# Idle TensorE products in the head of a macaron encoder layer, and its first loads in another order

## The chip, the core and the metric

One core of a Trainium2 chip runs the kernel. The time is that of one execution on the device, in microseconds (us); lower is better. The engines of the core run side by side, each with its own queue of instructions: TensorE (PE in the profile, PEld its weight loads) multiplies, VectorE (DVE) and ScalarE (ACT) do elementwise work, GpSimd (POOL) and SyncE (SP) mostly issue transfers (DMAs). An instruction waits at the head of its engine's queue until what it needs is there, and what is queued behind it waits too.

## What is computed

A layer on x of 1024 tokens by 1024 features, in float32: a half-step SwiGLU FFN, an attention block with two groups of heads, and a second half-step FFN, each between two RMS norms. The change touches only the start of the first FFN:

```python
def rmsnorm(x, g):
    xf = x.astype(jnp.float32)
    y = xf * lax.rsqrt(jnp.mean(xf * xf, axis=-1, keepdims=True) + NORM_EPS)
    return (y * g.astype(jnp.float32)).astype(x.dtype)

def swiglu(x, w_gate, w_up, w_down):
    return (jax.nn.silu(x @ w_gate) * (x @ w_up)) @ w_down
...
h = swiglu(rmsnorm(x, ffn1_pre_g[l]), ffn1_w_gate[l], ffn1_w_up[l], ffn1_w_down[l])
x = x + 0.5 * rmsnorm(h, ffn1_post_g[l])
```

## The kernel before

The matrix products run by a Strassen-like scheme on 512-wide blocks, and every operand is split into a rounded part (hi) and a rest (lo), so that one product of blocks is three matmuls: hi by hi (L466), hi by the rest of x (L467), rest by hi (L472). The four first tiles of x (128 rows each, 1024 columns) make the left operand of the first block.

The head does this. SP and ACT load tiles 0 and 1 of x in halves (L1637), the gain's row `ffn1_pre_g` (L1639, SP), then half blocks of two weights (L1647, L1651), tiles 2 and 3 of x (L1648 on ACT, L1649 on SP) and a third weight (L1652). The gain has to stand in all 128 partitions: `spread_gain` multiplies a row of ones (stationary, 1x128) by the gain's row (1x512, twice) on TensorE (L344, tile `gps`), and ACT copies the two results (L345). Meanwhile ACT and DVE square and sum the tiles (L166, L1665), and `rstd_by_sqrt` with `newton` make 1/rms for a pair of tiles (tile y, called r0 for tiles 0 and 1 and r1 for 2 and 3). `scaled` multiplies x by y and by the gain (L1672, tile xn), `transposed` turns it in blocks of 128x128 on TensorE (L174, tile trp), ACT rounds the result to hi (L181), DVE takes the rest (L182). Then the first products run (`pg.mm`, L466, L467, L472) on the columns of tiles 0 and 1 alone (256 wide). Tiles 2 and 3 follow with the same steps, and the products on the other 256 columns. ACT also splits the weights (L1683, with DVE L1686) and copies transposed blocks (L261) to be stored by POOL (L262).

In this head the order on TensorE, DVE and ACT is that in which the code is written (`ordered(DVE, ACT)`); SP and POOL issue their transfers in program order, and a transfer whose semaphore is still in use by an earlier one waits for it. The PSUM tiles of gps, of the products and of the tiles that the change adds come in turn from one pool of six banks (tag "mm"); those of the transposes have their own pool (L174).

`make_identity` fills c.ident (128x128), the stationary or moving operand of a transpose, on POOL at the start. xn[0] and xn[1] are the tiles that later hold the normalised tiles 0 and 1; before that, the gain's row lies in row 0 of xn[0] and the ones in xn[1].

Of the kernel before, what the change touches and what calls it, by code (L numbers as in the profile page):

```python
# [10 lines left out]
F32 = mybir.dt.float32  # L11
# [8 lines left out]
P, T = 128, 512  # L20
# [82 lines left out]
class Weights:  # L103
# [30 lines left out]
    def next(self):  # L134
        return self.ready.popleft()
# [180 lines left out]
def newton(c, y, e, h):  # L316

    nc = c.nc
    nc.vector.reciprocal(y, e)
    nc.vector.scalar_tensor_tensor(e, y, -1.0, h, op0=ALU.mult, op1=ALU.mult)  # L320
    nc.vector.tensor_mul(e, e, y)
    nc.vector.scalar_tensor_tensor(y, e, 1.5, y, op0=ALU.add, op1=ALU.mult)
    return y


def rstd_by_sqrt(c, ss):

    nc, k = c.nc, ss.shape[1]
    h, y, e = [c.small.tile([P, 4], F32, tag=t, name=t)[:, :k] for t in ("v", "y", "e")]
    nc.vector.tensor_add(h, ss[:, :, 0], ss[:, :, 1])  # L330
    nc.vector.tensor_scalar(h, h, 0.5 / D, 0.5 * EPS, op0=ALU.mult, op1=ALU.add)
    nc.scalar.activation(e, h, AF.Sqrt, scale=2.0)
    yield
    yield newton(c, y, e, h)


def spread_gain(c, t, row, one):

    nc = c.nc
    copies = []  # L340
    for h in range(2):
        sl = slice(h * T, h * T + T)
        ps = c.psm.tile([P, T], F32, tag="mm", name="gps")
        nc.tensor.matmul(ps, one, row[:, sl], start=True, stop=True)  # L344
        copies.append(lambda sl=sl, ps=ps: nc.scalar.copy(t[:, sl], ps))  # L345
    return t, *copies
# [1052 lines left out]
def layer(tc, a, out):  # L1399
    nc = tc.nc  # L1400
    c = Ctx(tc)
    with ExitStack() as ctx:
# [26 lines left out]
        x0 = [a["x"][t * P:(t + 1) * P, :] for t in range(8)]  # L1429
# [51 lines left out]
        def gate_pairs(which, op, wg, wu, early):  # L1481
            return PairGemm(c, op, [(wg[f], wu[f]) for f in range(NF)], early, GatePairs(c, which))

        def ffn(which, op, prep, pg, get, turns, sums, more, post, pre, src, dst, begin=None, tables=()):
# [7 lines left out]
            if begin:  # L1492
                left_pool(e)
            begun = begin(pg) if begin else ()
            plan(pg.early, turns)
            r = sub()
# [119 lines left out]
        with ExitStack() as order:  # L1616
# [9 lines left out]
            half = [slice(0, T), slice(T, D)]  # L1626
            first_junk = [c.xp.tile([P, D], F32, tag="s", name="junk", bufs=2)]
            w2 = c.xp.tile([P, D], F32, tag="x1", name="w2", bufs=2)
            xn = [c.xp.tile([P, D], F32, tag="xn", name="xn", bufs=c.xn) for _ in range(2)]
            gain = c.xp.tile([P, D], F32, tag="pre", name="gain", bufs=1)  # L1630
            xs = {t: c.xp.tile([P, D], F32, tag="x", name="x", bufs=4) for t in range(4)}
            xn += [xs[2], xs[3]]
            op0 = Operand(c, None, 0)
            nc.gpsimd.memset(xn[1][:1, :P], 1.0)
            for t in range(2):
                for h, q in enumerate((nc.sync, nc.scalar)):
                    q.dma_start(xs[t][:, half[h]], x0[t][:, half[h]])  # L1637
                    if (t, h) == (0, 0):
                        nc.sync.dma_start(xn[0][:1], a["ffn1_pre_g"])  # L1639
            op0.gain, *gains = spread_gain(c, gain, xn[0][:1], xn[1][:1, :P])  # L1640

            def begin(pg):
                for b in range(2):
                    pg.raw[b] = c.wg.tile([P, 2, T], F32, tag="g", name="graw")
                pg.raw[2] = w2.rearrange("p (i x) -> p i x", i=2)
                for b in range(2):
                    nc.sync.dma_start(pg.raw[b][:, 0], pg.srcs[b][0][:, half[0]])  # L1647
                nc.scalar.dma_start(xs[2], x0[2])  # L1648
                nc.sync.dma_start(xs[3], x0[3])  # L1649
                for b in range(2):  # L1650
                    nc.sync.dma_start(pg.raw[b][:, 1], pg.srcs[b][0][:, half[1]])  # L1651
# [6 lines left out]
                def square(t, h=None, to=None):  # L1658

                    x = xs[t] if h is None else xs[t][:, half[h]]  # L1660
                    acc = ss[t // 2][:, t % 2, h or 0:(h or 0) + 1]
                    if to is None:
                        sumsq(c, x, acc, junk()[:, :x.shape[1]])
                    else:
                        nc.vector.tensor_tensor_reduce(out=to, in0=x, in1=x, scale=1.0, scalar=0.0,  # L1665
                                                       op0=ALU.mult, op1=ALU.add, accum_out=acc)

                def scaled(r, h, *ts):

                    for t in ts:  # L1670
                        sl = half[h]
                        nc.vector.scalar_tensor_tensor(xn[t][:, sl], xs[t][:, sl], r[:, t % 2:t % 2 + 1],  # L1672
                                                       op0.gain[:, sl], op0=ALU.mult, op1=ALU.mult)
                        if not h:
                            op0.parts[t] = deque(((A11, xn[t][:, :T]), (A12, xn[t][:, T:])))
# [25 lines left out]
                gains[1]()  # L1701
                square(2)
                r0 = next(root)
                scaled(r0, 0, 0, 1)
                lo0(0)
                keeps = []
                op0.one(0, keeps)
                op0.one(1, keeps)
                hi1(0)
                square(3, 0)  # L1710
                square(3, 1, junk()[:, half[1]])
                root = rstd_by_sqrt(c, ss[1])
                next(root)
                lo1(0)
# [57 lines left out]
            pg = PairGemm(c, op, [(a["wqk"][p], a["wqk"][8 + p]) for p in QK_ORDER], 8, QKPairs(c))  # L1772
# [163 lines left out]
        with ordered():  # L1936
# [18 lines left out]
            pg = gate_pairs(3, op, a["wg2"], a["wu2"], 11)  # L1955
# [94 lines left out]
```

## Time and profile before

| what | value |
|---|---|
| median of 3 runs | 1828.1 us (1826.97 to 1828.38) |
| the profiled execution | 1828.32 us |
| its span, first to last instruction | 1826.5 us |
| mean granted TensorE clock | 0.999 |

The span in 40 equal slices (about 46 us each); each digit is the busy share in tenths, PEclk the granted TensorE clock, DMA the mean busy share of the 16 DMA engines:

```profile
PE   8999999999999999999999999999999999999998
PEclk9999999999999999999999999999999999999999
DMA  7756566557888858868687523594655566596564
```

TensorE is full but in the first and the last slice. The change works in the first 20 us, less than half of the first slice. A matmul's record is longer than its step: matmuls overlap, so the pace is read from start to start. A float32 product that isn't of the rounded kind (L344) leaves two records, each with a weight load.

### The profile page before, as it was taken

What the parts mean: (1) busy time and instruction counts of PE and PEld (TensorE: products, weight loads), DVE (VectorE), ACT (ScalarE), POOL (GpSimd) and SP (SyncE); (2) the same over time, 40 slices, a digit from 0 to 9 for tenths busy, and PEclk for the clock granted to TensorE, in tenths of its full rate; (3) what the DMA queues carried; (4) which work ended last, traced back from release to release, by engine and by line L of the source; (5) the groups of instructions that cost most, each with busy time, mean ns of one, the idle gap of its engine ahead of it and who ended that gap; (6) DMA issues with size and microseconds to landing.
All of it is one profiled execution on the core that took longest, in us unless ns stands there. A gap on an engine that the chain in (4) does not pass through costs nothing.

```text
span 1826.5 us, 25169 instructions
## 1 busy us (share of the span) xinstructions
PE 1808.7 (99%) x8876; PEld 1522.9 (83%) x8876; DVE 1309.8 (72%) x2225; ACT 832.1 (46%) x1495; POOL 352.3 (19%) x583
## 2 busy tenths in 40 slices
PE   8999999999999999999999999999999999999998
PEld 6888888888888888888999998888888888888886
DVE  6878877776466878477666856778877777664557
ACT  6622233334443656234688765654223333354433
POOL 2223321112021123232344100221111111110000
PEclk9999999999999999999999999999999999999999
DMA  7756566557888858868687523594655566596564
GB/s 277 263 182 215 166 226 224 203 208 260 306 302 307 288 200 265 265 226 294 198 264 254 184 97 116 192 309 162 196 179 196 201 221 223 185 349 196 193 230 143
DMA packets 172769, 409.28 MB, mean 224 GB/s; under 512 B 20401, under 2 KB 42321, under 8 KB 170594
## 3 DMA queue, kind: packets, MB, share of 16 engines
q1 hardware_dynamic: 124450, 246.07, 40.9%
q0 software_dynamic: 47184, 159.51, 24.0%
q10 hardware_dynamic: 1008, 2.10, 0.3%
q8 instruction: 70, 1.15, 0.3%
q14 instruction: 57, 0.47, 0.1%
HBM read 280.09 MB, written 132.56 MB: 226 GB/s over the span
## 4 chain that ended last, share of the span: by engine, by line
PE 92%; DVE 3%; DMA 2%; ACT 1%; issue 1%; SPq 0%; DVEq 0%; ACTq 0%
PE accp L783 26%; PE mmp L467 17%; PE mmp L466 17%; PE mmp L472 17%; PE po L1215 2%; PE ptp L1095 2%; PE po L1331 2%; PE accp L357 1%; PE accp L359 1%; PE accp L358 1%; PE sp L1182 1%; PE trp L174 1%; PE sp L1315 1%; DMA praw<-in_wd_dram 1%; DMA graw<-in_wg_dram 1%
## 5 line engine op out<-in xcount | busy, mean ns | idle before, releaser
L466 PE MATMUL mmp<-x,whi 128*128 128x512 f32 (+1 forms) x1464 | 571.8, 391 | 1.7 <-ACT x L181 1.4
L467 PE MATMUL mmp<-x,whi 128*128 128x512 f32 (+1 forms) x1464 | 569.2, 389 | 0.8 <-DVE x L182 0.7
L783 PE MATMUL accp<-pw 128*128 128x512 f32 x1800 | 411.2, 390 | 0.4 <-ACT hb L804 0.4
L783 PEld LDWEIGHTS accp<-pw 128*128 128x128 f32 x1800 | 337.2, 188 | 70.5 <-ACT hb L804 0.8
L472 PE MATMUL mmp<-x,wlo 128*128 128x512 f32 (+1 forms) x1464 | 390.6, 389 | 0.0
L466 PEld LDWEIGHTS mmp<-x,whi 128*128 128x128 f32 x1464 | 275.7, 188 | 59.6 <-ACT x L181 2.2
L467 PEld LDWEIGHTS mmp<-x,whi 128*128 128x128 f32 x1464 | 275.7, 188 | 57.4 <-DVE x L182 1.6
L472 PEld LDWEIGHTS mmp<-x,wlo 128*128 128x128 f32 x1464 | 274.7, 188 | 56.8
L751 DVE TENSOR_TENSOR pw<-praw,pw 128x1024 fp32r<-128x1024 f32 (+1 forms) x181 | 201.2, 1150 | 126.0 <-ACT pw L750 125.1
L750 ACT CAST pw<-praw 128x1024 fp32r<-128x1024 f32 (+1 forms) x181 | 168.8, 983 | 207.4 <-PE accp L783 162.6
L456 ACT CAST whi<-wraw 128x1024 fp32r<-128x1024 f32 x126 | 132.7, 1053 | 187.5 <-PE mmp L467 161.9
L457 DVE TENSOR_TENSOR wlo<-wraw,whi 128x1024 fp32r<-128x1024 f32 x126 | 153.3, 1218 | 2.5 <-ACT whi L456 2.5
L693 POOL DMA_DIRECT2D g<-sg x44 | 24.0, 545 | 428.5 <-DVE sg L686 243.0
L481 ACT COPY s<-mmp 128x512 f32<-128x512 f32 x52 | 30.6, 589 | 131.3 <-PE mmp L472 121.5
L456 ACT CAST whi<-traw 128x512 fp32r<-128x512 f32 x52 | 32.3, 621 | 122.9 <-DVE traw L554 100.0
L645 DVE TENSOR_TENSOR c<-mmp,u 128x512 f32<-128x512 f32 x52 | 35.9, 691 | 69.9 <-PE mmp L472 69.8
L553 DVE TENSOR_TENSOR wraw<-wraw 128x1024 f32<-128x1024 f32 x52 | 63.6, 1224 | 18.1 <-DMA wraw<-in_wu_dram 17.2
L783 PE MATMUL accp<-pw,x 128*128 128x512 f32 x312 | 71.8, 390 | 0.0
L1085 DVE CUSTOM_DVE_ANT_0 s<-sp,g 128x256 f32<-128x256 f32 (+1 forms) x128 | 48.3, 413 | 30.2 <-PE sp L1182 24.5
L783 PEld LDWEIGHTS accp<-pw,x 128*128 128x128 f32 x312 | 58.3, 188 | 12.4 <-DVE pw L751 0.3
L632 DVE TENSOR_TENSOR c<-mmp,v 128x512 f32<-128x512 f32 x52 | 35.8, 689 | 34.1 <-PE mmp L472 34.0
L1331 PE MATMUL po<-vs,pt 128*128 128x128 f32 x352 | 49.9, 276 | 0.0
(280 smaller groups left out, 2489.8 us busy)
## 6 DMA issues: line engine op xcount, KB each, us to landing
praw<-g SPq DMA_DIRECT2D x70, 512.0 KB
wraw<-in_wg_dram SPq DMA_DIRECT2D x44, 512.0 KB
wraw<-in_wu_dram SPq DMA_DIRECT2D x44, 512.0 KB
tr<-in_wd_dram SPq DMA_DIRECT2D x44, 512.0 KB
g<-sg POOLq DMA_DIRECT2D x88, 256.0 KB, 5.4
ts<-tr POOLq DMA_DIRECT2D x22, 1024.0 KB, 4.7
praw<-ts SPq DMA_DIRECT2D x88, 256.0 KB
praw<-in_wd_dram SPq DMA_DIRECT2D x66, 256.0 KB
```

The lines of the kernel that those rows point to most:

```text
L456: nc.scalar.copy(hi, raw)
L457: nc.vector.tensor_sub(lo, raw, hi.bitcast(F32))
L466: mm(out, hi[:, i, sl], xhi[:, k, cols], start=not go_on and k == 0, stop=False, skip_group_check=go_on)
L467: mm(out, hi[:, i, sl], xlo[:, k, cols], start=False, stop=False, skip_group_check=go_on)
L472: mm(out, lo[:, i, sl], xhi[:, k, cols], start=False, stop=k == 3, skip_group_check=go_on)
L553: nc.vector.tensor_sub(r[:, 0:2], r[:, 1:3], r[:, 0:2])
L750: nc.scalar.copy(hi, raw[:, :m])
L751: nc.vector.tensor_sub(lo, raw[:, :m], hi.bitcast(F32))
L783: c.nc.tensor.matmul(acc[t], a, b, start=not chained and gi == 0 and j == i == 0, stop=end and j + n >= len(ops) and i == len(two) - 1, sk ...
L1085: c.nc.vector.tensor_tensor_reduce(out=s, in0=ps, in1=bias, scale=-1.0, scalar=3e38, op0=ALU.add, op1=ALU.min, accum_out=neg)
L1095: nc.tensor.transpose(ps[:, j, :], src[:, j * P:(j + 1) * P], c.ident)
L1331: nc.tensor.matmul(po[0][:, u], pt[0][:, j, :], vs[:, k0 + j, :], start=j == 0, stop=j == n - 1)
```

## The change

It adds a helper that issues n products of a 128x128 tile by itself into a PSUM tile that nothing reads, and calls it four times: 8 products ahead of the norm's two, on the tile of ones; 9 behind them, on the identity; 4 behind a small product of the identity by two columns of r0 (which makes them wait for r0), ahead of the first transposes; 2 behind those transposes. The norm's two products now take all 128 rows: the ones fill xn[1][:, :128], and xn[0] is set to zero by DVE ahead of the gain's row, which lands in its first row. That row is now loaded by POOL's queue, and tile 2 of x by SP's, between the first halves of the two weights.

```diff
+def turn_over(c, x, n):
+
+    ps = c.psm.tile([P, P], F32, tag="mm", name="idle")
+    for _ in range(n):
+        c.nc.tensor.matmul(ps, x, x, start=True, stop=True)
...
-            nc.gpsimd.memset(xn[1][:1, :P], 1.0)
+            nc.gpsimd.memset(xn[1][:, :P], 1.0)
+            nc.vector.memset(xn[0], 0.0)
             for t in range(2):
                 for h, q in enumerate((nc.sync, nc.scalar)):
                     q.dma_start(xs[t][:, half[h]], x0[t][:, half[h]])
-                    if (t, h) == (0, 0):
-                        nc.sync.dma_start(xn[0][:1], a["ffn1_pre_g"])
-            op0.gain, *gains = spread_gain(c, gain, xn[0][:1], xn[1][:1, :P])
+            nc.gpsimd.dma_start(xn[0][:1], a["ffn1_pre_g"])
+            turn_over(c, xn[1][:, :P], 8)
+            op0.gain, *gains = spread_gain(c, gain, xn[0], xn[1][:, :P])
+            turn_over(c, c.ident, 9)
...
-                for b in range(2):
-                    nc.sync.dma_start(pg.raw[b][:, 0], pg.srcs[b][0][:, half[0]])
-                nc.scalar.dma_start(xs[2], x0[2])
+                nc.sync.dma_start(pg.raw[0][:, 0], pg.srcs[0][0][:, half[0]])
+                nc.sync.dma_start(xs[2], x0[2])
+                nc.sync.dma_start(pg.raw[1][:, 0], pg.srcs[1][0][:, half[0]])
                 nc.sync.dma_start(xs[3], x0[3])
...
                 r0 = next(root)
+                nc.tensor.matmul(pg.bank()[:, :2], c.ident, r0[:, :2], start=True, stop=True)
+                turn_over(c, c.ident, 4)
                 scaled(r0, 0, 0, 1)
                 lo0(0)
                 keeps = []
                 op0.one(0, keeps)
                 op0.one(1, keeps)
+                turn_over(c, c.ident, 2)
                 hi1(0)
```

TensorE's first instructions before (line, operation, out<-in, size, how many in a row; gps is the spread gain, trp the transposes, mmp the products):

```order
L344 MATMUL gps<-xn 128x512 x2
L174 MATMUL trp<-ident,xn 128x128 x8
L466 MATMUL mmp<-x_161,whi 128x256
L467 MATMUL mmp<-x_162,whi 128x256
L466 MATMUL mmp<-x_161,whi 128x256
```

and in the changed kernel, at the same place:

```order
L341 MATMUL idle<-xn 128x128 x8
L351 MATMUL gps<-xn 128x512 x2
L341 MATMUL idle<-ident 128x128 x9
L1713 MATMUL mmp<-y,ident 128x2
L341 MATMUL idle<-ident 128x128 x4
L174 MATMUL trp<-ident,xn 128x128 x8
L341 MATMUL idle<-ident 128x128 x2
L473 MATMUL mmp<-x_161,whi 128x256
```

Eight products stand ahead of gps, 9 + 4 and the one with r0 (y) between gps and the transposes, 2 behind these; all that follows on TensorE is in the order of before.

SP's first transfers before (x are the tiles of x, graw and w the raw weights, xn the gain's row):

```order
L1637 DMA x<-in_x_dram 128x512
L1639 DMA xn<-in_ffn_pre_g_dram 1x1024
L1637 DMA x<-in_x_dram 128x512
L1647 DMA graw<-in_wg_dram 128x512 x2
L1649 DMA x<-in_x_dram 128x1024
L1651 DMA graw<-in_wg_dram 128x512 x2
L1652 DMA w_153<-in_wg_dram 128x1024
```

and in the changed kernel:

```order
L1645 DMA x<-in_x_dram 128x512 x2
L1655 DMA graw<-in_wg_dram 128x512
L1656 DMA x<-in_x_dram 128x1024
L1657 DMA graw<-in_wg_dram 128x512
L1658 DMA x<-in_x_dram 128x1024
L1660 DMA graw<-in_wg_dram 128x512 x2
L1661 DMA w_153<-in_wg_dram 128x1024
```

The gain's row is gone from this queue, and tile 2 has come in (L1656). ACT's queue keeps its two halves of tiles 0 and 1. On POOL the row stands behind the identity's making and ahead of two small memsets:

```order
L1641 MEMSET xn 128x128
masks.py:199 ISA
masks.py:199 AFFINE_SELECT ident<-ident 128x128
L1646 DMA xn<-in_ffn_pre_g_dram 1x16x64
L1700 MEMSET ss_239 128x4
L1700 MEMSET ss_240 128x4
```

This transfer waits for DVE's memset of xn, the first instruction on DVE now. No other instruction has changed its place on an engine.

## The prediction

> **What bounds the kernel now.** The page first: TensorE is busy for nearly the whole span, so only what stands ahead of its unbroken run can move the end. Then the waits of TensorE after 26 us, to see where that run begins.
>
> ```profile
> span 1826.5 us, 25169 instructions
> PE 1808.7 (99%) x8876; PEld 1522.9 (83%) x8876; DVE 1309.8 (72%) x2225; ACT 832.1 (46%) x1495; POOL 352.3 (19%) x583
> PE mmp L466 <- ACT x L181: 0.7, 1, 0.7
> PE trp L174 <- DVE og L1380: 0.4, 1, 0.4
> ```
>
> The largest wait of TensorE after 26 us is 0.7 us, and the next is 0.4 us: from 28.29 us on it hardly stops. Its later work is fed by transfers that start when earlier work frees a buffer, so what the head gains or loses before that point reaches the end whole. The chain of work in order of time shows the head (start, length, what).
>
> ```profile
> 1.56 4.57 DMA x<-in_x_dram
> 6.15 0.72 ACT junk L166 x2
> 6.87 0.47 ACT gain L345
> 8.41 0.76 DVE xn L1672
> 9.31 1.96 PE trp L174 x8
> 11.28 0.59 ACT x L181
> 11.90 0.70 DVE x L182
> 12.65 0.58 PE mmp L467
> ...
> 16.64 0.71 PE trp L174 x4
> 17.38 0.60 ACT x L181
> 17.99 1.30 DVE x L182 x2
> 19.34 0.39 PE mmp L467
> ```
>
> The end is set by a chain: the last half of x's tile 1 (rows 128 to 255) lands, is squared (6.15), normalised (8.41), transposed (9.31), split into a rounded part on ACT and a rest on DVE, and multiplied (12.65). From 19.34 to 26.9 us TensorE leads again, with no long wait. So I follow one thing: when the second pair of tiles (2 and 3) lets TensorE go on, now 19.34.
>
> The pace of TensorE within this head, from the timeline and from the instructions of line 174 in the first 20 us (min/median/max in ns):
>
> ```profile
> 13.03 0.41 PE L466 MATMUL mmp<-x,whi 128*128 128x256 f32 x1
> 13.24 0.41 PE L467 MATMUL mmp<-x,whi 128*128 128x256 f32 x1
> ...
> 19.56 0.28 PE L466 MATMUL mmp<-x,whi 128*128 128x256 f32 x1
> 19.68 0.28 PE L467 MATMUL mmp<-x,whi 128*128 128x256 f32 x1
> L174 PE MATMUL trp<-ident,xn x8: 421/421/448, 9.3 to 10.8; 128*128 128x128 f32 x8
> L174 PE MATMUL trp<-ident,x x8: 272/273/421, 16.4 to 17.5; 128*128 128x128 f32 x8
> 16.86 0.80 PE L174 MATMUL trp<-ident,x 128*128 128x128 f32 x5
> 17.18 0.60 PE L174 MATMUL trp<-ident,x 128*128 128x128 f32 x4
> ```
>
> The same 256-column product starts every 0.21 us at 13 us and every 0.12 us at 19.6 us. The transposes change too, from 421 to 272 ns, and the starts (16.86 plus one step of 0.21, then 17.18) put the change at about 17.07 us. The granted clock doesn't show it (1.00 in the windows before and behind, below); I call the two paces slow and full. TensorE had then run without a gap since 12.65: 17.07 - 12.65 = 4.42 us.
>
> **The change part by part.** *Products nothing reads.* 8 + 9 + 4 stand ahead of the transposes of the first pair, 2 behind them. None is in the trace. The norm's own products are the nearest rows:
>
> ```profile
> 4.40 3.75 PE L344 MATMUL gps<-xn 1*128 1x512 f32 x4 [4.40 <-DMA xn<-in_ffn_pre_g_dram]
> L344 PE MATMUL gps<-xn x4: 1056/1056/1187, 4.4 to 7.1; 1*128 1x512 f32 x4
> ```
>
> Two products of 512 columns are four records and take some 3.5 us at the slow pace from start to start (4.4 to 7.1 are three steps, 0.9 each). An idle product has 128 columns, so two records like a transpose's 0.213: 0.427 us slow, 0.213 full. Below, a free pass is excluded, since the array takes products in order; above, the four-record row gives 0.9 x 2 / 4 = 0.45. I take 0.427. Counting a gps product as four such units, 8 + 8 + 9 + 4 = 29 units stand ahead of the first transpose, 12.4 us slow and 6.2 us full. The product with r0 has two columns; by a transpose step for each record it costs 0.2 us.
>
> *When they start.* The first eight wait only for a memset on POOL, which was there before, on one row instead of 128:
>
> ```profile
> 0.89 0.20 POOL L1634 MEMSET xn<- 1x128 f32 x1
> L960 POOL MEMSET neg<- x1: 441/441/441, 129.5 to 129.5; 128x384 f32 x1
> tt<-in_t_rel_bias_dram POOLq DMA_DIRECT2D x1, 1.0 KB, 2.9
> DMA to landing us min/median/max: 2.2/3.3/5.4
> ```
>
> The number of rows costs an elementwise engine nothing while the columns stay, so it ends at 1.1 and TensorE starts at 1.2. The eight last until 1.2 + 3.4 = 4.6.
>
> *The gain's row.* It goes from SP's queue to POOL's, behind a new DVE memset of 128x1024. POOL's two memsets (195 ns for 128 columns, 441 for 384) give 0.96 ns a column, so an estimate of 1.06 us; DVE has nothing else to do there and can begin when POOL does its memset (0.89), so only the row waits for it: issue at 1.9. Behind this wait on POOL stand the two memsets of ss, then needed at 3.45 by ACT, and ready by 2.7: nothing lost. POOL's small loads land 2.2 to 5.4 us after issue (the last row above, of the bias stacks; the other of 1 KB took 2.9): 4.1 to 7.3, I take 4.8. Before, TensorE waited for it until 4.40. So TensorE has a gap of 0.2 us.
>
> *When the pace changes.* Dense work from 1.2 plus the measured 4.42 gives 5.6 us. Both ends: if the pace were full at once, the transposes would wait for xn as now; if it never changes, 1.2 + 12.4 + 0.4 = 14.0. With a change at time X, the units by X take 0.427 and the rest half of it, so the first transpose starts at 0.5 X + 7.1 (0.1 for the gap, 0.2 for r0's product). X = 5.6 gives 9.9, against 9.31 now: the idle products hold it back by 0.6 us, though xn is there.
> The Trainium skill's "TensorE: Matmul & The Clock Gate", in "What's actually happening", says that the array runs at half rate until a free-running window of about 3.4 us was busy. By it X lies 3.4 to 6.8 us behind the dense start, at 4.6 to 8.0, and my sum below would be between 1.5 us gained and 0.1 us lost. The same page's Part 4 says that the full rate doesn't engage for transposes; that would take 0.44 us from the gain, but the 421 and 272 ns rows speak against it.
>
> *From the first transpose to 19.34.* Call its start t. Rows of the second pair, at full pace, give the steps: four transposes 0.44, then 0.2 to ACT (17.18 to 17.38), and 19.34 - 17.38 = 1.96 from ACT's start to the product with the rest. So the first product with the rest starts at t + 2.6, where it was 9.31 + 3.34. The 17 products after it take 17 x 0.12 = 2.0, and no longer hold the second pair back. That pair then waits for DVE and ACT:
>
> ```profile
> 12.51 0.68 DVE L1665 CUSTOM_DVE_ANT_0 junk<-x 128x512 f32<-128x512 f32 x1
> 14.96 1.42 DVE L1672 SCALAR_TENSOR_TENSOR x<-x,y,gain 128x512 f32<-128x512 f32 x2
> 15.36 1.06 ACT L261 COPY raw<-trp 128x512 f32<-128x512 f32 x2
> ```
>
> On ACT, 4.55 us lie between the end of the last first-pair cast (the chain's 11.28 + 0.59 = 11.87) and the end of the copies (16.42). The casts of the first pair end at t + 0.64 + 2 x 0.6 = t + 1.87, so ACT is free at t + 6.42 and needs 1.96 more: t + 8.38. DVE agrees: squares from t + 2.55, tile 2 scaled 3.1 us later, tile 3 at t + 6.34, its four transposes and 0.2 until t + 7.0, when ACT has just ended tile 2's cast. So 19.34 becomes t + 8.38: **the break-even is t = 10.96**, and t = 9.9 gains 1.06 us. The two idle products behind the transposes (0.43 us) end at t + 1.3, ahead of ACT's cast: nothing. The four behind r0 are in t.
>
> *The loads.* Tile 2 of x moves from ACT's queue to SP's, between the first halves of the two weights, and tile 3 no longer waits for the first load to land.
>
> ```profile
> 8.07 0.62 ACT L1683 CAST whi<-graw 128x512 fp32r<-128x512 f32 x1 [0.56 <-DMA graw<-in_wg_dram]
> 10.00:12.00 2.00, 1.32 (x7) 0.93 (x5) 1.21 (x3) 1.53 (x5) 0.00 (x0) 1.00 1.02 405
> 12.00:14.00 2.00, 1.85 (x7) 1.56 (x8) 1.86 (x6) 1.30 (x5) 0.00 (x0) 1.00 0.04 16
> ```
>
> The last two rows are windows (their last columns are granted clock, DMA share and GB/s). The bytes stay and the DMA engines are full until 12 us, so the last load ends as before. The wait of 0.56 us should go, and the left half of tile 1, issued one place sooner (1.56 was its start, with the row's issue ahead of it, so some 0.4 us), lets xn begin up to 0.4 earlier. With t set by TensorE at 9.9 this is worth nothing; where the pace changes early, up to 0.4. If tile 2 came late, its square would start late on ACT, ahead of the casts; it has the third place behind 1 MB of tiles 0 and 1 and 0.25 MB of weight, 0.5 MB itself, and at the 405 GB/s of the window these 1.75 MB take 4.3 us; the squares on ACT that stand ahead of it end at 6.9 now, so it lies some 0.5 us beside them from a first byte at 2.1.
>
> **Sum.** 1828.32 (the profiled execution: the span and 1.8 around it) - 1.06 = 1827.26. The median 1828.1 lies 0.2 below that execution, so 1827.0.
>
> **The rivals.**
> 1. *The row lands late (slower).* For it: POOL's path under full DMA engines, up to 5.4 us; against it: the medians. TensorE stops at 4.6 and is dense only from the landing. If the 4.42 us count anew from there, 21 units are left: t = landing + 4.42 + (21 - 10.35) x 0.2135 + 0.2 = landing + 6.9, so it decides from the first landing behind 4.6 whose gap counts (t = 11.5, 0.5 lost); whether 0.2 us count, no row tells. 5.4 gives t = 12.3 and +1.3 (1829.4), 7.3 gives +3.2 (1831.3).
> 2. *The idle products don't change the pace.* For it: the one-row products ran for 3.75 us and left it slow. Against it: 4.42 us of full-row products changed it. Then t = 14.0, the first pair is slow as now, and the head is 14.0 - 9.31 = 4.7 us late: 1832.8.
> 3. *No net change.* The pace changes at about 7.7 us, t = 10.96, and the gain in the first products is paid by the queue of idle ones: 1828.1.
> 4. *More.* The pace changes by 4 us, t follows xn at 9.31 - 0.4 = 8.9: 2.0 gained, 1826.1.
>
> **How the numbers follow.** Forecast 0.58, rivals 0.20, 0.04, 0.10 and 0.08. 0.2% is 3.7 us, about what a measurement of this kernel can tell from no change; even rival 4 stays inside, and rival 2 alone lies outside for certain. Faster 0.02 (a gain nobody has named here), slower 0.06 (rival 2 and the far end of rival 1), the same 0.92. The range holds the forecast, rivals 3 and 4 and the nearer two thirds of rival 1, with 0.5 us for the spread of the runs: 1825.6 to 1830.3.
>
> **What would show it.** Right: idle products at steps of 0.43 first and 0.21 later, the change near 5.6 us; first transposes at about 9.9, 0.11 apart; the first product with the rest near 12.5, the next ones 0.12 apart; the second pair's at 18.3. Wrong: a gap of TensorE ahead of gps of 0.5 us or more, a pace that falls back between the transposes and the products, first transposes behind 10.96, or an end that doesn't follow the head's shift within 0.5 us.

## The result and the profile after

| | before | changed kernel |
|---|---|---|
| median (6 runs each, side by side) | 1828.24 us (1826.97 to 1829.43) | 1834.86 us (1832.27 to 1838.17) |
| ratio | 1 | 1.0036, 95% interval 1.0026 to 1.0046 |
| profiled execution | 1828.32 us | 1832.27 us |
| its span | 1826.5 us | 1830.5 us |

The kernel became 6.6 us slower in the median. A second comparison (experiment e14) gave 1834.10 against 1828.92, ratio 1.0025 (1.0015 to 1.0036). The profiled execution is the fastest of the six and shows 4.0 us of the loss.

First the page of the changed kernel, then its waits of TensorE after 26 us (us in all, times, longest).

```profile
span 1830.5 us, 25267 instructions
PE 1812.0 (99%) x8924; PEld 1527.8 (83%) x8924; DVE 1311.9 (72%) x2226; ACT 832.4 (45%) x1495; POOL 350.9 (19%) x584
PE mmp L473 <- ACT x L181: 0.7, 1, 0.7
PE mmp L473 <- ACT s L488: 0.6, 1, 0.6
PE po L1338 <- DVE pt L1104: 0.6, 1, 0.6
```

TensorE is as full as before, and no single wait behind 26 us is long enough to hold 4 us, which points to the head. The last stall of the head, a wait for the rest of x (L182), is the mark for the head's end. A second mark lies near 1040 us, at transposes of the attention's output. Both in the trace of before, and then in that of the changed kernel:

```profile
28.29 0.50 PE L467 MATMUL mmp<-x,whi 128*128 128x512 f32 x1 [0.23 <-DVE x L182]
1039.19 0.63 PE L174 MATMUL trp<-ident,og 128*128 128x128 f32 x4 [0.41 <-DVE og L1380]
```

```profile
32.16 0.50 PE L474 MATMUL mmp<-x,whi 128*128 128x512 f32 x1 [0.22 <-DVE x L182]
1044.28 0.63 PE L174 MATMUL trp<-ident,og 128*128 128x128 f32 x4 [0.42 <-DVE og L1387]
```

The head ends 32.16 - 28.29 = 3.87 us later, and the span is 4.0 us longer. The stretch between the marks grew from 1010.90 to 1012.12 us; behind the second mark 1.1 us comes back. The two nearly cancel, so within these two executions the head is the loss.

The chain of work of the changed kernel in order of time (start, length, what) names the cause.

```profile
1.03 0.92 DVE xn L1642
1.95 0.29 issue
2.24 5.80 DMA xn<-in_ffn_pre_g_dram
8.04 0.14 issue
8.18 3.48 PE gps L351 x4
11.66 2.01 PE idle L341 x18
13.67 0.12 PE mmp L1713 x2
13.79 1.00 PE idle L341 x8
14.79 0.45 PE trp L174 x4
```

Before, the chain began with tile 1 of x. Now it begins with the gain's row: zeroed tile, issue on POOL's queue at 2.24, landing at 8.04. Then the norm's products, and behind them the idle ones stand ahead of the transposes. TensorE's timeline shows what the gap did:

```profile
1.14 3.61 PE L341 MATMUL idle<-xn 128*128 128x128 f32 x16 [1.14 <-POOL xn L1641]
8.18 3.48 PE L351 MATMUL gps<-xn 128*128 128x512 f32 x4 [3.43 <-DMA xn<-in_ffn_pre_g_dram]
11.50 2.17 PE L341 MATMUL idle<-ident 128*128 128x128 f32 x18
...
14.62 1.04 PE L174 MATMUL trp<-ident,xn 128*128 128x128 f32 x8
15.49 0.61 PE L341 MATMUL idle<-ident 128*128 128x128 f32 x4
...
17.22 0.38 PE L474 MATMUL mmp<-x,whi 128*128 128x256 f32 x1 [0.45 <-DVE x L182]
17.44 0.28 PE L473 MATMUL mmp<-x,whi 128*128 128x256 f32 x1
17.56 0.28 PE L474 MATMUL mmp<-x,whi 128*128 128x256 f32 x1
...
20.56 1.26 PE L174 MATMUL trp<-ident,x 128*128 128x128 f32 x8 [1.05 <-ACT raw L261]
...
23.23 0.38 PE L474 MATMUL mmp<-x,whi 128*128 128x256 f32 x1 [0.34 <-DVE x L182]
```

The idle products do what they were put there for: the first transposes and products run at the full pace (0.12 us from start to start). But TensorE stands still for 3.43 us ahead of gps, the first transposes come at 14.62 instead of 9.31, and the second pair's product at 23.23 instead of 19.34: 3.9 us, the head's loss. The wait of 1.05 us for ACT's copies (L261) is new: at the full pace TensorE is through the products of the first pair by about 19.5, and the copy that frees the first PSUM tile for the transposes ends only at 20.5, behind ACT's splits of the weights. In before both copies had ended at 16.42, and the slow products lasted as long, to 16.44.

Windows of the same trace (us, busy time of PE, PEld, DVE, ACT and POOL, then granted clock, DMA share, GB/s):

```profile
6.00:8.00 2.00, 0.00 (x0) 0.00 (x0) 1.03 (x4) 0.67 (x2) 0.00 (x0) 0.96 0.97 336
8.00:10.00 2.00, 1.82 (x2) 0.84 (x3) 0.00 (x0) 0.00 (x0) 0.00 (x0) 0.50 1.02 383
10.00:12.00 2.00, 2.00 (x8) 1.18 (x7) 0.81 (x5) 1.50 (x4) 0.00 (x0) 0.68 1.05 415
```

Here the granted clock does show the pace: 0.50 from 8 to 10 us, while gps ran slow. By that, 0.96 over 6 to 8 us is 0.16 us at half rate, so the pace fell at about 7.84; 0.68 over 10 to 12 is 1.28 us at half rate, so it was full again at 11.28. The full pace had been reached before that (the idle records of 1.14 to 4.75 go from 421 ns down to 274), it was lost in the gap, and gps ran slow, 3.48 us.

### The profile page after: what moved, and what is told of

It reads as the page before. It is cut to its first block, busy times and chain, and to the rows that moved or that the text cites. A ratio compares the mean times of both kernels' runs of the same rounds, so it can differ in the third digit from the quotient of the medians.

```text
span 1830.5 us, 25267 instructions
## 1 busy us (share of the span) xinstructions
PE 1812.0 (99%) x8924; PEld 1527.8 (83%) x8924; DVE 1311.9 (72%) x2226; ACT 832.4 (45%) x1495; POOL 350.9 (19%) x584
## 4 chain that ended last, share of the span: by engine, by line
PE 91%; DVE 3%; issue 2%; DMA 2%; ACT 1%; POOL 1%; DVEq 0%; POOLq 0%; ACTq 0%; SPq 0%
PE accp L790 26%; PE mmp L479 17%; PE mmp L473 17%; PE mmp L474 17%; PE po L1222 2%; PE ptp L1102 2%; PE po L1338 2%; PE sp L1189 1%; PE accp L364 1%; PE accp L366 1%; PE accp L365 1%; PE sp L1322 1%; PE trp L174 1%; DMA x<-xn 0%; DMA rg<-ob 0%
## 5 line engine op out<-in xcount | busy, mean ns | idle before, releaser
L790 PEld LDWEIGHTS accp<-pw,x 128*128 128x128 f32 x312 | 58.3, 188 | 12.3 <-DVE pw L758 0.3
```

Of the source, the lines that this page charges most:

```text
L790: c.nc.tensor.matmul(acc[t], a, b, start=not chained and gi == 0 and j == i == 0, stop=end and j + n >= len(ops) and i == len(two) - 1, sk ...
```

## The experiments

All runs stand beside runs of the kernel before on the same chip. "Row used" is the start of the norm's products, t that of the first transposes, "head" the first mark (28.29 in before), "stretch" the time from the first mark to the second. These four are of one profiled execution; the median's difference and the ratio are of all runs.

| kernel | row used | t | head | stretch | median - before | ratio (95%) |
|---|---|---|---|---|---|---|
| before, first profile | 4.40 | 9.31 | 28.29 | 1010.90 | | |
| before, again (e15) | 4.39 | 8.96 | 28.35 | 1011.54 | one run, 1829.11 | |
| changed kernel | 8.18 | 14.62 | 32.16 | 1012.12 | +6.6 | 1.0036 (1.0026-1.0046) |
| changed kernel again (e14) | 8.34 | 14.78 | 32.31 | 1012.21 | +5.2 | 1.0025 (1.0015-1.0036) |
| e1 row by SP, third | 5.54 | 12.36 | 29.89 | 1014.21 | +2.2 | 1.0016 (1.0007-1.0025) |
| e13 row by SP, ninth | 11.97 | 18.64 | 36.17 | 1012.85 | +9.2 | 1.0051 (1.0033-1.0069) |
| e2 before, row by POOL | 7.45 | 12.01 | 31.20 | 1010.39 | +2.2 | 1.0012 (1.0003-1.0022) |
| e3 change, no idle products | 8.39 | 12.95 | 30.86 | 1010.31 | +1.6 | 1.0012 (1.0003-1.0021) |
| e4 before, idle products | 4.86 | 11.62 | 29.16 | 1012.56 | +3.3 | 1.0018 (1.0008-1.0027) |
| e16 the same again | 4.80 | 12.52 | 30.77 | 1014.09 | one run, 1832.83 | |
| e6 e4, one PSUM tile more | 4.86 | 10.02 | 27.58 | 1012.79 | +2.9 | 1.0009 (1.0000-1.0019) |
| e11 e4, tile 2 by SP | 4.85 | 14.07 | 31.61 | 1013.95 | +1.4 | 1.0008 (0.9999-1.0017) |
| e12 seven idle products | 4.51 | 10.48 | 28.78 | 1015.50 | +1.1 | 1.0005 (0.9995-1.0014) |
| e10 first eight alone | 4.86 | 9.45 | 28.07 | 1012.30 | +0.1 | 0.9999 (0.9990-1.0009) |
| e9 before, tile 2 by SP | 4.40 | 9.35 | 28.67 | 1012.31 | -1.1 | 0.9996 (0.9986-1.0006) |
| e5 before, PSUM tiles turned | 4.06 | 11.43 | 30.66 | 1010.52 | -0.3 | 0.9995 (0.9985-1.0004) |
| e7 change, one PSUM tile more | 8.04 | 15.76 | 33.30 | 1012.12 | +3.8 | 1.0023 (1.0013-1.0032) |
| e8 e1, one PSUM tile more | 6.79 | 13.37 | 30.90 | 1012.72 | +2.2 | 1.0013 (1.0004-1.0023) |

### The row alone, and the change without it

e1: the changed kernel with the row issued by SP behind the two halves of x.

```diff
-            nc.gpsimd.dma_start(xn[0][:1], a["ffn1_pre_g"])
+            nc.sync.dma_start(xn[0][:1], a["ffn1_pre_g"])
```

> The changed kernel, but the gain's row is issued by SP behind the two tile halves (start at about 2.0 us, when DVE's memset is done) instead of by POOL. Theory (the row's late landing costs the time): it lands at about 5 to 6.5 us instead of 8.1, the pace stays full from about 4.5 on, the first transpose starts at 9.5 to 10.7, and the kernel ends at 1826.6 to 1827.9. Rival (the 23 idle products themselves cost the time, by standing ahead of the transposes): no better than 1832 to 1835. Second rival (the new order of the weights and tile 2 costs it): likewise 1832 to 1835.

The row was used 2.6 us earlier, and the head ended 2.3 us earlier:

```profile
5.54 3.75 PE L351 MATMUL gps<-xn 128*128 128x512 f32 x4 [0.62 <-DMA xn<-in_ffn_pre_g_dram]
```

The head is still 1.6 us late and the median 2.2 us above before's: the queue was part of the loss, not all of it. Neither expectation came out. The median, 1831.33, lies between those of the theory and of its rivals, and t is 12.36 instead of 9.5 to 10.7, because the pace was not full from 4.5 us on: the norm's four records ran slow (5.54 to 9.29).

e2: the kernel before with nothing but the row on POOL's queue.

```diff
-                    if (t, h) == (0, 0):
-                        nc.sync.dma_start(xn[0][:1], a["ffn1_pre_g"])
+            nc.gpsimd.dma_start(xn[0][:1], a["ffn1_pre_g"])
```

> The kernel before with one edit: the gain's row is loaded by POOL's queue, with no memset to wait for (issue at about 1.4 us); no idle products, one-row products of the norm. Theory (late landing): the row lands at 6.5 to 8 us and the head slips by 2 to 4 us: 1830 to 1832. Rivals (idle products or the loads' order cost it): 1828.2, as before.

The row is issued at 1.5 here, no zeroing ahead of it, and lands no sooner than 7.3 (rows: start of the issue, then from issue to landing, then gps):

```profile
L1638 POOL DMA_DIRECT2D xn<-in_ffn_pre_g_dram x1: 664/664/664, 1.5 to 1.5; - x1
DMA to landing us min/median/max: 5.8/5.8/5.8
7.45 3.75 PE L344 MATMUL gps<-xn 1*128 1x512 f32 x4 [7.45 <-DMA xn<-in_ffn_pre_g_dram]
```

So the 5.8 us are those of a small load on POOL's queue at this place, with or without the change's other parts. SP's queue at the same place took 3.4 us in e1 and 4.7 in e8 (both issued at 1.97), under DMA engines as full (share from 2 to 8 us 0.99 in e1, 0.95 in e2), so the queue has a share in it. Alone the late row costs 2.9 us of head and 2.2 us of median.

e3: the changed kernel without its idle products and without the product by r0.

```diff
-            turn_over(c, xn[1][:, :P], 8)
...
-            turn_over(c, c.ident, 9)
...
-                nc.tensor.matmul(pg.bank()[:, :2], c.ident, r0[:, :2], start=True, stop=True)
-                turn_over(c, c.ident, 4)
...
-                turn_over(c, c.ident, 2)
```

> The changed kernel without its 23 idle products and without the product that waits for r0; the row stays on POOL's queue behind the memset, and the norm's two products keep their full rows. Theory (late landing): the row lands at 8 us or later; the first transpose starts at about 12.7 and the products behind it go at the slow pace, so 3.4 us are lost in a run that lands at 8: 1831 to 1834, within 1.5 us of the changed kernel. Rival (the idle products cost it): 1828.2 or less.

With the row as late as in the change (8.39) the head ends at 30.86, 1.3 us earlier than with the idle products. So behind a late row they cost time: they stand ahead of the transposes (12.95 here, 14.62 there) and give back only a part. The median, 1830.72, is just under the expected 1831 to 1834 and 3.4 to 4.1 us below the changed kernel's, where at most 1.5 was expected: the idle products' share is larger than the theory had it.

e13: the changed kernel with the row where it was written before, and the zeroing shared by two engines.

```diff
-            nc.vector.memset(xn[0], 0.0)
+            nc.vector.memset(xn[0][:, half[0]], 0.0)
+            nc.gpsimd.memset(xn[0][:, half[1]], 0.0)
...
+                    if (t, h) == (0, 0):
+                        nc.sync.dma_start(xn[0][:1], a["ffn1_pre_g"])
-            nc.gpsimd.dma_start(xn[0][:1], a["ffn1_pre_g"])
```

> The changed kernel with the gain's row back at its old place on SP's queue, second after the first half of tile 0, and the zeroing of its tile shared by DVE and POOL (half the columns each), so that the row is issued early. All else is as in the change: full rows, all idle products, tile 2 on SP's queue. Theory (the late row on POOL's queue is the main loss): the row lands by 4.9 us, TensorE has no gap ahead of the norm's products and runs densely from 1.14 us; since the dense time that came before a change of pace was 3.4 to 5.5 us in the traces so far, the pace changes between 4.6 and 6.6, the first transposes start at 9.4 to 10.5, the head ends 0 to 1 us before the 28.29 of the kernel before, and the median is 3 to 5 us below the changed kernel's in the same call. Rival (the idle products and the queue of tile 2 cost it, wherever the row lands): the head ends early all the same but the median is within 1.5 us of the changed kernel's.

It did the opposite, and is the clearest run of all. First SP's queue, then gps on TensorE:

```profile
4.25 0.90 SPq L1662 DMA_DIRECT2D graw<-in_wg_dram  x2
5.89 0.31 SPq L1648 DMA_DIRECT2D xn<-in_ffn_pre_g_dram  x1
```

```profile
11.97 3.71 PE L351 MATMUL gps<-xn 128*128 128x512 f32 x4 [7.04 <-DMA xn<-in_ffn_pre_g_dram]
```

The row, written second, stands ninth in the built queue, behind eight loads (why it was put there, no run shows). It was used 3.8 us later than in the change, t came 4.0 and the head 4.0 us later, and the median rose 4.0 us above the changed kernel's beside it (1838.11 against 1834.10). The expectation had the row early and falls with it, but the dose is the answer: between these two kernels, alike behind the row, the end follows the row nearly one for one.

e7 and e8: the changed kernel and e1 with one more PSUM tile that nobody uses, so that all later products have the banks of before.

```diff
                 turn_over(c, c.ident, 2)
+                c.psm.tile([P, T], F32, tag="mm", name="place")
```

> The changed kernel with one unused PSUM tile more, so that the turn of the banks stands as before. Its trace is also a second look at the row's landing on POOL's queue. Theory A: 1.5 to 2.5 us faster than the changed kernel, which leaves the late row's 3 to 4 us: 1831 to 1833. Theory B: as the changed kernel, 1833 to 1837. In both the row lands at 7 us or later.

> The changed kernel with the row on SP's queue behind the two tile halves, and one unused PSUM tile more. Theory A: 1.5 to 2.5 us faster than the same without that tile, so level with the kernel before. Theory B: no change by the tile, 2 to 3 us slower than before. The row lands at about 5.5 us.

The heads end 1.1 and 1.0 us later than without the tile, the medians are 3.8 and 2.2 us above before's. For e8 that is what e1 has. For e7 it is less than the changed kernel's 5.2 and 6.6, but the intervals overlap, so a gain by the tile is neither shown nor excluded there. In e7 the idle products ran slow from 1.14 to 4.9 and again behind gps, which is where its first 1.1 us went. In e8 the row was used at 6.79 instead of the expected 5.5, from the same issue as in e1, which is where its 1.0 us went.

### The idle products with an early row

e4: the kernel before with the idle products (and ones in all rows) alone; the row keeps its queue.

```diff
-            nc.gpsimd.memset(xn[1][:1, :P], 1.0)
+            nc.gpsimd.memset(xn[1][:, :P], 1.0)
+            turn_over(c, xn[1][:, :P], 8)
             op0.gain, *gains = spread_gain(c, gain, xn[0][:1], xn[1][:1, :P])
+            turn_over(c, c.ident, 9)
...
+                nc.tensor.matmul(pg.bank()[:, :2], c.ident, r0[:, :2], start=True, stop=True)
+                turn_over(c, c.ident, 4)
...
+                turn_over(c, c.ident, 2)
```

> The kernel before with the idle products alone (8, 9, 4 and 2, and the product with r0); the row stays on SP's queue at its old place, the norm's products keep one row, the loads their old order. Theory (late landing): the row lands at 4.4 as before, the pace is full from 4.5 to 8 us on, the first transpose starts at 9.3 to 10.5: a gain of 0.5 to 1.6 us, 1826.6 to 1827.7. Rival (the idle products cost it): 1832 to 1835.

e6: the same and one PSUM tile more.

```diff
                 turn_over(c, c.ident, 2)
+                c.psm.tile([P, T], F32, tag="mm", name="place")
```

> The idle products alone on the kernel before (row on SP, old loads), with one unused PSUM tile more, so that the turn of the six banks stands as before. Theory A (turn of the banks): the waits at 688 and 893 us go, and the time falls from 3 us above the kernel before to its level or 1 us below. Theory B (shift against the transfers): as without the tile, 2 to 3.5 us slower than before, the waits for DVE's rest at 80 us and for ACT's copy at 688 us still there.

e11: e4 with tile 2 of x on SP's queue.

```diff
-                for b in range(2):
-                    nc.sync.dma_start(pg.raw[b][:, 0], pg.srcs[b][0][:, half[0]])
-                nc.scalar.dma_start(xs[2], x0[2])
+                nc.sync.dma_start(pg.raw[0][:, 0], pg.srcs[0][0][:, half[0]])
+                nc.sync.dma_start(xs[2], x0[2])
+                nc.sync.dma_start(pg.raw[1][:, 0], pg.srcs[1][0][:, half[0]])
```

> The kernel of before with all the idle products and with tile 2 of x on SP's queue as in the change; the gain's row keeps its old place on SP's queue and the norm's own products keep one row. So it is the change without the late row. Theory (late row and a loss of 1.5 to 2 us behind the head that idle products bring, apart): the row lands by 5 us, the first transposes start at 9.6 to 10.2, the head ends 0.5 to 1 us earlier than before's 28.29, the stretch behind it to the transposes at about 1039 is 1012 to 1014 us, and the median is within 1 us of before's, on the slow side. Rival (the late row is the whole loss): the stretch is 1010.3 to 1010.9, and the median is 1 us or more below before's.

TensorE begins alike in all three. Here are e6 and then e11:

```profile
4.86 2.00 PE L351 MATMUL gps<-xn 1*128 1x512 f32 x4
...
18.65 0.38 PE L474 MATMUL mmp<-x,whi 128*128 128x256 f32 x1 [0.34 <-DVE x L182]
```

```profile
4.85 3.78 PE L351 MATMUL gps<-xn 1*128 1x512 f32 x4
8.56 4.21 PE L341 MATMUL idle<-ident 128*128 128x128 f32 x18
```

The same four records, from the same start behind the same eight products, take 2.00 us in e6 and 3.78 in e11: in e6 the pace changed at about 5 us, in e11 not before 12.8, and t is 10.02 or 14.07. With this early change the head of e6 ends 0.71 us before that of before; with the late one that of e11 3.3 us behind it, so its expected t fell while its stretch (1013.95) came out as expected. Its median is 1.4 us above before's, with an interval that just holds 1. In e4 tile 1's half landed at 8.2 and held t at 11.62. e4 once more (e16) gave a third course:

> The kernel of before with all idle products once more (nothing else of the change but ones in all rows of their tile). In its first profile the pace changed at 5.4 us, in two kernels with the same first instructions on TensorE not before 8.6. If the change's place is each execution's own, it lies elsewhere now, and the norm's four records end anywhere from 6.8 to 8.6 us. The stretch from the head's end to the transposes near 1039 us was 1012.6 us; 1012 to 1014 again would fit a loss that idle products bring, 1010 to 1011 an accident of one execution.

```profile
6.00:8.00 2.00, 2.00 (x13) 1.29 (x12) 0.00 (x0) 0.00 (x0) 0.00 (x0) 1.00 0.98 319
8.00:10.00 2.00, 1.69 (x9) 1.39 (x8) 0.82 (x5) 1.98 (x6) 0.00 (x0) 0.52 0.98 373
10.00:12.00 2.00, 1.77 (x8) 1.78 (x9) 1.89 (x4) 1.42 (x3) 0.00 (x0) 0.50 1.04 415
12.00:14.00 2.00, 2.00 (x11) 2.00 (x11) 0.29 (x1) 0.38 (x1) 0.00 (x0) 0.50 0.14 55
14.00:16.00 2.00, 1.66 (x9) 1.33 (x8) 1.60 (x3) 1.73 (x4) 0.00 (x0) 0.77 0.00 0
```

The pace was full early, as in e6 (gps took 1.98 us), and then lost. 0.52 over 8 to 10 us puts the loss at 8.08, and 0.77 over 14 to 16 the return at 14.92. At 8.08 TensorE had no gap behind it; but up to 6.7 the norm's one-row products had run. In the stretch that follows it stood still for 0.5 us at 9.7, since y was late (tile 1's half landed at 8.0, below). In e4, the same kernel, it was not lost, though TensorE stood still for 1.1 us at 9.3. So where the pace changes, and whether it lasts, differs between executions of one kernel. The runs scatter accordingly: e6 has three of ten at 1828.1 to 1829.1 us and seven at 1832.0 to 1833.7, and its profile is the fastest of them.

e10: the first eight idle products alone. e12: only those behind r0 and behind the transposes.

```diff
+            turn_over(c, xn[1][:, :P], 8)
             op0.gain, *gains = spread_gain(c, gain, xn[0][:1], xn[1][:1, :P])
```

> The kernel of before with the first eight idle products alone (and ones in all rows of their tile); the norm's own products have one row, as before, and no idle products follow. Kernels with all idle products took 1012.1 to 1014.2 us from the end of the head to the transposes at about 1039 us, those without 1010.3 to 1010.9. Theory 1 (the loss comes with the head that TensorE runs through at the full pace): the norm's one-row products leave the pace slow, so the first transposes are slow and the head ends as in before (28.3, or 30.3 to 30.7 if the half of tile 1 lands at 8.2), and the stretch behind is 1010.3 to 1010.9. Theory 2 (it comes with the number of instructions added to TensorE's queue, eight of the 23 here): the stretch behind is 1011 us or more with the same head.

```diff
+                nc.tensor.matmul(pg.bank()[:, :2], c.ident, r0[:, :2], start=True, stop=True)
+                turn_over(c, c.ident, 4)
...
+                turn_over(c, c.ident, 2)
```

> The kernel of before with the product by r0, the four idle products behind it and the two behind the first transposes alone: seven products instead of 24, placed so that TensorE is dense from about 8.5 us. Theory 1 (the loss behind the head comes with a head that TensorE runs at the full pace): the first transposes start at about 10.2, the pace is full by about 13, the head ends about 0.5 us earlier (if the half of tile 1 is in time), and the stretch behind it to the transposes at about 1039 us is 1012 us or more. Theory 2 (the number of added instructions): the head is the same, the stretch is 1011 to 1011.5. If neither holds, it is 1010.3 to 1010.9 and the median is 0.5 to 1 us below before's.

The eight alone, which lie in TensorE's first idle 4 us, cost nothing and bring nothing (0.9999). The seven give t = 10.48, a full pace only from 14.3, and no gain. Neither theory of the stretch holds in both: e10 has the old head and a stretch of 1012.30, against theory 1; e12 has the fewest products and the longest stretch, against theory 2.

### Loads and banks without idle products

e5: the kernel before with five PSUM tiles that nobody uses. e9: the kernel before with tile 2 on SP's queue, as in e11.

```diff
                 r0 = next(root)
+                for _ in range(5):
+                    c.psm.tile([P, T], F32, tag="mm", name="place")
```

> The kernel before with five PSUM tiles of the pool of six taken and never used, at the place where the idle products take theirs: no idle product, no moved load, only each later product one bank further back in the turn, as in the changed kernel. Theory A (the turn of the banks costs time, since the kernels with idle products wait 0.6 to 0.7 us for ACT's copy at 688 us and others don't): slower than before by 1 to 2.5 us, with that wait in its trace. Theory B (the idle products cost by shifting TensorE against the transfers of the head): same as before within 0.5 us, no such wait.

> The kernel of before with one part of the change: tile 2 of x goes from ACT's queue to SP's, between the first halves of the two weights; the gain's row stays where it was, no idle products. In the kernels with ACT's old order the left half of tile 1 landed at 6.1 us in two profiles and at 8.2 us in two others, with the same loads. Theory (the order of the loads decides that half): it lands by 6.3 us, the first transposes start at 9.1 to 9.3, the head ends (the last stall of TensorE, 28.29 in before) within 0.3 us of 28.3, and the median is 0.5 to 1.5 us below before's because its late landings are gone. Rival (the half lands early or late by chance in either order): it lands at about 8.2 in some of the runs, and the median is within 0.5 us of before's. Behind the head, with no idle products, both expect the 1010.3 to 1010.9 us up to the transposes at about 1039 us that the other kernels without them took.

ACT's square of tile 1's left half in e5 (in e9 it starts at 6.20):

```profile
8.27 0.63 ACT L166 ACTIVATE junk<-x 128x512 f32<-128x512 f32 x1 [2.82 <-DMA x<-in_x_dram]
```

Turning the banks costs nothing (0.9995), though this profile's head is 2.4 us late: the half landed at 8.27. With ACT's old order it came at 6.2, 5.8, 6.1, 6.0 and 5.8 (before, e15, e6, e10, e12) and by 5.5 in e2, but at 8.2, 8.0 and 8.3 in e4, e16 and e5; in the nine profiles with tile 2 on SP never behind 6.6. That the order decides it isn't shown: e9's median is 1.1 us below before's, and its interval holds 1. Its head (28.67) and its stretch (1012.31) came out above the expected ones. No version beat the kernel before by more than the runs scatter.

### The two kernels again

> The changed kernel once more, beside the one with the row at its old place. If the row's landing on POOL's queue is the kernel's and not one execution's, it lands at 7.4 to 8.5 us again, the norm's products start there, the first transposes at landing + 6.4 to 7.7 and the head ends 3 to 5 us behind the 28.29 of the kernel before. If it was one execution's, it lands by 6 us. Where the pace changes should differ from the first profile (4.55, back at 7.96, full again at 11.37), if the phase of that change is each execution's own.

> The kernel before once more. If the place at which the pace changes and the landing of tile 1's left half are each execution's own, one or both differ from the first profile: change at 17.07, 4.42 us behind the start of dense work, and landing at 6.15; the half may land at 8.2 and the head then ends at 30.3 to 30.7. If they are the kernel's, the head ends at 28.3 again. The stretch from the head's end to the transposes near 1039 us was 1010.9; if it moves by over 1 us, what the kernels differ by there (1010.3 to 1015.5) is mostly the execution's.

The row landed late again (from issue to landing 6.0 us), the pace was lost in the gap again, the head ended at 32.31. The late row belongs to the kernel. The pace was expected to change elsewhere and did not: the granted clock of 1.00, 0.50 and 0.65 in the windows from 6 to 12 us puts its loss at 8.00 and its return at 11.40, against 7.84 and 11.28. Before ended its head at 28.35, with t 0.35 us earlier and a stretch 0.64 us longer. There the pace did change elsewhere: the second pair's transposes, up to 17.6 us, still ran slow (421 ns), where in the first profile the change came at 17.07.

## Why the prediction was wrong

**What bounds the kernel: right for this pair, not in general.** The head's shift (3.87) and the span's (4.0) agree within 0.13 us, and e13 moved them by 4.0 and 4.5 more. But that a shift of the head "reaches the end whole" fails in other kernels: the head moved by 1.60 and the span by 3.7 in e1, by 0.49 and 4.9 in e12, by 2.57 and 0.9 in e3. What lies behind the head takes part, and the prediction put it at nothing.

**The failed step: the gain's row.** The prediction put its landing at "4.1 to 7.3, I take 4.8", from small loads on POOL's queue at other times. It landed at 8.04, 5.80 us after its issue, past the far end; in all five profiles with this load on POOL's queue the norm's products started between 7.45 and 8.39. The range itself was misread: its 5.4 is not of a small load. That row of tile stk mixes the eight loads of 11 KB (2.3 to 3.7 us) with sixteen of 48 KB that write from stk (2.2 to 5.4). And the small loads were issued under less load. The one of 1 KB that took 2.9 us was issued at 126.3 us (start of its issue below), where the DMA share is 0.64, against 0.96 from 2 to 8 us (window's last columns: clock, DMA share, GB/s).

```profile
L938 POOL DMA_DIRECT2D tt<-in_t_rel_bias_dram x1: 529/529/529, 126.3 to 126.3; - x1
126.00:130.00 4.00, 4.00 (x20) 3.30 (x19) 3.65 (x6) 1.69 (x2) 3.92 (x8) 1.00 0.64 204
2.00:8.00 6.00, 3.60 (x4) 1.16 (x4) 1.42 (x7) 4.00 (x8) 0.00 (x0) 1.00 0.96 340
```

The prediction's own text named "POOL's path under full DMA engines" and gave it 0.20. Small loads on this queue took 2.3 to 3.7 us between 111 and 129 us, and 5.7 to 6.0 here; e1 and e8 show that the queue has a share in it, but what the full engines add to a load on this queue, no run shows by itself. The row also had to wait for the zeros, which the full-row products need: 2.24 instead of 1.2, behind all first halves (the prediction had 1.9). e1 shows that SP's queue at that place gives 5.54, so even there the gap is 0.62 us.

**Rival 1: its form was right, its closeness partly luck.** t = landing + 6.9 gives 14.9 for 8.04, measured 14.62; for e1 (landing at 5.41) 12.3, measured 12.36; for e8 (6.66) 13.6, measured 13.37; for e13 (about 0.14 us ahead of its use at 11.97) 18.7, measured 18.64; but for e7 (7.91) 14.8, measured 15.76. The 4.42 us in it are no constant: the full pace came back 3.1 us behind the start of the norm's products in the changed kernel and 4.5 us behind it in e8 (0.98, 0.50 and 0.67 in the windows from 6 to 12 us put the return at 11.32). With 10.96 as break-even the changed kernel loses 14.94 - 10.96 = 3.98 us: 1832.30 for the profiled execution, which took 1832.27. There two errors cancel. The measured t is 0.3 us earlier, and the break-even lies 0.2 us earlier too: from t to the second pair's product it is 8.61 us (14.62 to 23.23, in e1 12.36 to 20.97), where the sum had 8.38.

**Second failure: the pace as a fixed delay, and with it the gain of the idle products.** The prediction put the change at "1.2 plus the measured 4.42". That delay was one execution's. In before once more (e15) the pace was still slow over 5 us behind 12.31, the start of its dense work. e6 and e11, alike up to there, changed some 4 us and over 11 us after their start, and e16 changed twice. That the one-row products between them don't count as dense work fits e11 and e16, and e10, where the pace stayed slow through them; it was not tested by itself. The Trainium skill, "TensorE: Matmul & The Clock Gate" ("What's actually happening"), has a free-running window of about 3.4 us. The trace agrees in its length: 7.84 to 11.28 is 3.44 us, 8.00 to 11.40 in e14 is 3.40, 8.08 to 14.92 in e16 is twice 3.42. The start of these steps differs between executions in e4 and e16, one kernel, but hardly between the two profiles of the changed kernel. The prediction had this rule beside its sum and used it for X alone, not for the loss of the pace in a gap, nor for the scatter that it means.

**Right where its condition held.** In e6, with the row early and the pace changing at about 5 us, t was 10.02 (forecast 9.9), the second pair's product came at 18.65 (forecast 18.3), and the head gained 0.71 us (forecast 1.06). Nothing of it is seen in the median: e6 +2.9, e4 +3.3, e11 +1.4.

**The row is not the whole of the median's loss.** The late row without idle products costs 1.6 to 2.2 us (e3, e2), against 5.2 and 6.6 for the changed kernel. The idle products with the row early cost 3.3, 2.9 and 1.4 us (e4, e6, e11, the last with an interval that holds 1), where the prediction had them gain 1.06. Of the 3.87 us of head in the profiled pair, 2.57 come with the late row alone (e3), and 1.30 with the products that stand behind it. So the median needs both.

**The part that stays open.** The changed kernel's profile explains 4 of the 5.2 to 6.6 us. In the changed kernel, in e4 and in e6 the profile is the fastest or second fastest execution, so the scatter of the pace may hold part of the rest; that is not shown. Besides, the stretch behind the head is 1012.1 to 1015.5 us in the twelve profiles with idle products and 1010.3 to 1011.5 in five of the six without (e9: 1012.3). The extra waits are single ones of up to 1.9 us (e12, at 1017.59, for DVE's pt). Behind the second mark some 0.7 us comes back on average. Neither the turn of the PSUM banks (e5, e6, e7, e8) nor the full pace in the head (e10) nor the number of added products (e12) explains it; what does is not settled.

**The chances.** Slower by over 0.2% had 0.06, because rival 1 stopped at a landing of 7.3, and because rival 2, idle products that bring nothing, had 0.04. A rival must be followed past the rows at hand when the condition it rests on, here full DMA engines, is harsher than in the rows that were read.

## What to carry to other kernels

Where TensorE is filled with products that nobody reads to raise its pace, everything they stand in front of, and the one transfer that they surround, decides much: look first at the smallest load on the path, and price it by loads on the same queue that were issued into equally full DMA engines. Keep such a load on the queue and at the place where it was early; a form that needs a zeroed tile ahead of the load gives that place up. And a gain that depends on when the pace changes is a gain of some executions: compare several, not one profile.

## What was not expected of the hardware

- A load of 4 KB issued by POOL between 1.5 and 2.2 us took 5.7 to 6.0 us to land while the DMA share was 0.9 and more (five profiles); the issue from SP at 1.2 landed by 4.4, those at 1.97 took 3.4 and 4.7 us, and that at 5.89 took until 11.97.
- One-row products for 3.78 us left the pace slow (e11), though TensorE was dense from 1.14 us on, and in e16 the full pace was lost 1.4 us behind them.
- The granted clock shows the slow pace at the start of a program as 1.00, and as 0.50 once the pace has been full and was lost (e16: 0.50 in the windows from 10 to 14 us).
